# Norm factors spread by transposes, a shorter square-root chain, and latent norms taken half by half

## The chip, the cores and the metric

The kernel runs on one core of a Trainium2 chip. The metric is the device time in microseconds (us) of one execution of the whole program. A profile is taken of one execution, which has a time of its own.

## The reference

Two layers of a hybrid encoder are applied to 544 tokens (512 of a new stream, 32 of a running one). Cut to what matters here:

```
def rmsnorm(x, g):
    return x * rsqrt(mean(x * x, axis=-1) + EPS) * g

def mixer(h, ...):
    b_g, c_g, xin, q_lat, ckv, k_r, g_a, g_b = split(h @ w_in)
    y_a = (b_g * conv(c_g * xin)) @ w_conv_out
    q = rmsnorm(q_lat, norm_q) @ w_uq        # 384 features; then RoPE on a part
    c_new = rmsnorm(ckv, norm_kv)            # 256 features; also an output
    y_b = attention(q, c_new @ w_ukv, rope(k_r)) @ w_attn_out
    return (sigmoid(g_a) * y_a + sigmoid(g_b) * y_b) @ w_merge

def layer(x, ...):
    x = x + rmsnorm(mixer(rmsnorm(x, norm_attn_pre)), norm_attn_post)
    f = (silu(gate(h2)) * up(h2)) @ w_down   # h2 = rmsnorm(x, norm_ffn_pre)
    return x + rmsnorm(f, norm_ffn_post)
```

So each layer has four norms over 1024 features and two over the latents (384 and 256 features). Each needs one factor 1/sqrt(mean square + EPS) per token.

## The kernel before

Features lie on the 128 partitions and tokens along the free dimension. The tokens are worked in two halves of TH = 272 columns (`hf` 0 and 1). A product of a weight tile with a half is three matmuls, since both operands are split into a high and a low part (L184: low part of the weights, L185: low part of the data, L186: both high parts). Weights come as raw tiles of 512 KB by DMA from SP's queue; ACT copies out the high part (L129) and DVE subtracts to get the low part (L130). A unit is one output tile of 128 features for one half: 8 input tiles times 3, that is 24 products of 272 columns.

Each layer begins with the input projection. Its first part, units (m, hf) with m = 0 to 7 for half 0 and then for half 1, makes the query latent (m = 0 to 2), the key and value latent (m = 3, 4) and more; `p1_evict` copies each unit out of PSUM and adds its squares to `accq` or `acck` of its half. Then come the convolution branch, RoPE, attention, merge, gate and up, and down.

A norm factor is made in two steps. `rsqrt_cols` (L231) takes accumulators of squares, 128 partitions by 272 tokens. Three products per accumulator with one column of `ones` (L237, at token offsets `TB3` = 0, 128, 144) put the sums over the features on the partitions as three columns. DVE scales them (L239), makes a first guess `y` by integer arithmetic on the bits (L242) and improves it by three Newton steps of three operations (L244 to L246), all on tiles 128 by 3 per accumulator. Then it multiplies the identity by each column: three diagonal tiles `dg` per accumulator (L251). `bcast` (L255) multiplies `ones` with these tiles (L259: 128, 128 and 16 columns) and so spreads the factor over all partitions in PSUM, where DVE uses it.

`first_chain` (L388) does this once per half for the input, and `post_chain` (L320) twice per half after the merge and after the down projection (the norm on the way out and the next one on the way in; after the last projection there is no next one): 16 single spreads into the bank ring `v`. `qk_norms` (L506) does all four latent accumulators at once, 12 columns, after unit (6, 1) of each layer's first part. Their four spreads, two in ring `s` and two in ring `t`, follow one another a little later (L635 to L648), ahead of the products that need the normalised latents.

The order of PE's, SP's and POOL's instructions is that of the code. For DVE and ACT it is that of the code in the first layer's first part and from the merge to the end of the next layer's first part; elsewhere a scheduler orders them. PSUM's eight banks are rings: `d` 3, `s` 2, `t` 2, `v` 1. In the first part the call for the next bank, `psd`, goes round through `d`, `s` and `t` in a fixed order, for units and for the columns of `rsqrt_cols` alike.

Of the kernel before, what the change touches and what calls it, by code (L numbers as in the profile page):

```python
# [11 lines left out]
ALU = mybir.AluOpType  # L12
AX = mybir.AxisListType

P = 128
NL = 2
T = 544
TH = 272
# [5 lines left out]
EPS = 1e-6  # L24
QSCALE2 = 96.0
# [3 lines left out]
TB3 = (0, 128, 144)  # L29
# [4 lines left out]
def kernel(  # L34
# [25 lines left out]
    pe, dve, act, pool = nc.tensor, nc.vector, nc.scalar, nc.gpsimd  # L60
# [22 lines left out]
    def small(shape, dt=F32, s="s"):  # L83
        return sp.tile(shape, dt, tag="s", name=nm(s))

    def tiny(shape, s="y"):
        return sp.tile(shape, F32, tag="y", name=nm(s), bufs=16)
# [143 lines left out]
    def rsqrt_cols(accs):  # L231
        n = 3 * len(accs)
        ps = psd(n)
        v = tiny([P, 12], "v")[:, :n]
        for i, (acc, scale, eps) in enumerate(accs):
            for b, o in enumerate(TB3):
                pe.matmul(ps[:, 3 * i + b : 3 * i + b + 1], lhsT=acc.t[:, o : o + P], rhs=ones[:, 0:1], start=True, stop=True)  # L237
        for i, (acc, scale, eps) in enumerate(accs):
            dve.tensor_scalar(v[:, 3 * i : 3 * i + 3], ps[:, 3 * i : 3 * i + 3], scale, eps, op0=ALU.mult, op1=ALU.add)  # L239
        y = tiny([P, 12], "y")[:, :n]  # L240
        t = tiny([P, 12], "t")[:, :n]
        dve.tensor_scalar(y.bitcast(I32), v.bitcast(I32), -0.5, float(0x5F3759DF), op0=ALU.mult, op1=ALU.add)  # L242
        for _ in range(3):
            dve.tensor_mul(t, y, y)  # L244
            dve.scalar_tensor_tensor(t, t, -0.5, v, op0=ALU.mult, op1=ALU.mult)
            dve.scalar_tensor_tensor(y, t, 1.5, y, op0=ALU.add, op1=ALU.mult)  # L246
        out = []
        for i in range(len(accs)):
            d = small([P, TH], s="dg")
            for b, (o, a) in enumerate(((0, 0), (P, 0), (2 * P, 112))):  # L250
                dve.tensor_scalar_mul(d[:, o : min(o + P, TH)], ident[:, a:P], y[:, 3 * i + b : 3 * i + b + 1])  # L251
            out.append(d)
        return out

    def bcast(d, tag="v"):  # L255
        ps = bank(tag)[:, :TH]
        for o in (0, P, 2 * P):
            e = min(o + P, TH)
            pe.matmul(ps[:, o:e], lhsT=ones, rhs=d[:, o:e], start=True, stop=True)  # L259
        return ps  # L260

    FS = 1.0 / (NC * P)
# [190 lines left out]
    for l in range(NL):  # L453
# [26 lines left out]
        accq = [Acc(), Acc()]  # L480
# [20 lines left out]
                if m < 5:  # L501
                    (accq if m < 3 else acck)[hf].add(dst)

        qk = []

        def qk_norms():  # L506
            qk.extend(rsqrt_cols([(acck[0], 1.0 / 256, EPS), (acck[1], 1.0 / 256, EPS),
                                  (accq[0], QSCALE2 / 384, EPS * QSCALE2), (accq[1], QSCALE2 / 384, EPS * QSCALE2)]))

        if l == 0:  # L510
            pend = []

            def evict(n):
                for _ in range(n):
                    p1_evict(*pend.pop(0))
# [9 lines left out]
                (7, 0): lambda: evict(1),  # L525
                (1, 1): lambda: (next(norm_b), next(norm_a)),
                (3, 1): lambda: (next(norm_b), evict(4)),
                (4, 1): lambda: evict(1),
                (5, 1): lambda: evict(1),
                (6, 1): lambda: (evict(1), qk_norms()),  # L530
                (7, 1): lambda: (evict(1), next(norm_b)),
            }

# [11 lines left out]
        else:  # L545
            pend = []
            for m, hf, ps in win_tiles(range(8), 8, P1Src(h, raws)):
                pend.append((m, hf, ps))
                if hf == 0 or hf in sready:
                    while pend:  # L550
                        p1_evict(*pend.pop(0))
                tick()
                if (m, hf) == (6, 1):
                    qk_norms()
            while 1 not in h:
                step()
            while loaded:
# [645 lines left out]
```

## Time and profile before

| what | us |
|---|---|
| three runs: lowest, median, highest | 2022.95, 2024.89, 2026.08 |
| the profiled execution | 2026.63 |
| its span, first to last instruction | 2024.6 |
| PE busy in the span | 1992.8 |
| DVE busy in the span | 1147.1 |

The profiled execution took 2.0 us more than its span, and 1.74 us more than the median of the runs. PE has work in nearly the whole span. Its mean granted clock is 0.994 of full speed.

### The profile page before, as it was taken

What the parts mean: (1) busy time and instruction counts of PE and PEld (TensorE: products, weight loads), DVE (VectorE), ACT (ScalarE), POOL (GpSimd) and SP (SyncE); (2) the same over time, 40 slices, a digit from 0 to 9 for tenths busy, and PEclk for the clock granted to TensorE, in tenths of its full rate; (3) what the DMA queues carried; (4) which work ended last, traced back from release to release, by engine and by line L of the source; (5) the groups of instructions that cost most, each with busy time, mean ns of one, the idle gap of its engine ahead of it and who ended that gap; (6) DMA issues with size and microseconds to landing.
All of it is one profiled execution on the core that took longest, in us unless ns stands there. A gap on an engine that the chain in (4) does not pass through costs nothing.

```text
span 2024.6 us, 37375 instructions
## 1 busy us (share of the span) xinstructions
PE 1992.8 (98%) x15588; PEld 1970.8 (97%) x15588; DVE 1147.1 (57%) x2410; ACT 827.2 (41%) x1676; POOL 85.7 (4%) x212
## 2 busy tenths in 40 slices
PE   8999999999999999999999999999999999999997
PEld 8999999999999999999999999999999999999997
DVE  7877776534467444422668777864344664444234
ACT  5455555622353223222444555556123533222231
POOL 0100000000000000000100100100000000000000
PEclk9999999999999999999999999999999999999998
DMA  5122222222342222232532222222223412222233
GB/s 192 62 77 68 69 82 69 92 97 84 116 150 84 84 84 84 84 97 86 184 105 77 65 65 75 88 83 88 84 94 118 158 55 93 85 95 81 79 115 125
DMA packets 58890, 190.92 MB, mean 94 GB/s; under 512 B 7969, under 2 KB 9665, under 8 KB 58593
## 3 DMA queue, kind: packets, MB, share of 16 engines
q1 hardware_dynamic: 49104, 163.58, 24.1%
q0 software_dynamic: 8320, 22.66, 3.4%
q8 instruction: 122, 2.00, 0.4%
q10 hardware_dynamic: 1296, 2.29, 0.3%
q14 instruction: 48, 0.39, 0.1%
HBM read 174.11 MB, written 10.20 MB: 91 GB/s over the span
## 4 chain that ended last, share of the span: by engine, by line
PE 93%; DVE 4%; DMA 1%; ACT 1%; issue 1%; SPq 0%; DVEq 0%; ACTq 0%
PE ps_d L184 16%; PE ps_d L186 16%; PE ps_d L185 16%; PE ps_s L184 7%; PE ps_s L186 7%; PE ps_s L185 7%; PE ps_t L184 6%; PE ps_t L186 6%; PE ps_t L185 6%; PE ps_t L757 2%; DMA raw<-in_w_in 1%; PE ps_v L772 1%; PE ps_v L773 1%; DVE w L130 1%; ACT w L129 1%
## 5 line engine op out<-in xcount | busy, mean ns | idle before, releaser
L130 DVE TENSOR_TENSOR w<-raw,w 128x1024 fp32r<-128x1024 f32 (+4 forms) x317 | 363.8, 1148 | 433.5 <-ACT w L129 432.5
L129 ACT CAST w<-raw 128x1024 fp32r<-128x1024 f32 (+4 forms) x317 | 312.1, 986 | 263.3 <-PE ps_d L186 109.4
L184 PE MATMUL ps_d<-hh,w 128*128 128x272 f32 x1080 | 314.9, 292 | 1.3 <-DVE v L130 1.3
L185 PE MATMUL ps_d<-hl,w 128*128 128x272 f32 x1080 | 312.0, 289 | 0.8 <-DVE hl L314 0.8
L186 PE MATMUL ps_d<-hh,w 128*128 128x272 f32 x1080 | 312.1, 289 | 0.0
L184 PE MATMUL ps_d<-gh,w 128*128 128x272 f32 x704 | 205.9, 292 | 6.0 <-DVE w L130 6.0
L184 PEld LDWEIGHTS ps_d<-hh,w 128*128 128x128 f32 x1080 | 203.8, 189 | 3.0 <-PE ps_d L186 1.7
L185 PEld LDWEIGHTS ps_d<-hl,w 128*128 128x128 f32 x1080 | 203.5, 188 | 2.0 <-DVE hl L314 1.3
L186 PE MATMUL ps_d<-gh,w 128*128 128x272 f32 x704 | 204.5, 291 | 0.0
L185 PE MATMUL ps_d<-gl,w 128*128 128x272 f32 x704 | 203.5, 289 | 0.0
L186 PEld LDWEIGHTS ps_d<-hh,w 128*128 128x128 f32 x1080 | 203.1, 188 | 0.0
L184 PEld LDWEIGHTS ps_d<-gh,w 128*128 128x128 f32 x704 | 133.3, 189 | 6.5 <-DVE w L130 6.3
L184 PE MATMUL ps_s<-gh,w 128*128 128x272 f32 x464 | 136.9, 295 | 1.1 <-DVE w L130 1.1
L186 PE MATMUL ps_s<-gh,w 128*128 128x272 f32 x464 | 136.1, 293 | 0.0
L185 PE MATMUL ps_s<-gl,w 128*128 128x272 f32 x464 | 135.4, 292 | 0.0
L185 PEld LDWEIGHTS ps_d<-gl,w 128*128 128x128 f32 x704 | 133.6, 190 | 0.0
L186 PEld LDWEIGHTS ps_d<-gh,w 128*128 128x128 f32 x704 | 133.3, 189 | 0.0
L184 PE MATMUL ps_t<-gh,w 128*128 128x272 f32 x432 | 125.5, 290 | 0.0
L186 PE MATMUL ps_t<-gh,w 128*128 128x272 f32 x432 | 125.0, 289 | 0.0
L185 PE MATMUL ps_t<-gl,w 128*128 128x272 f32 x432 | 124.3, 288 | 0.0
L1051 ACT ACTIVATE sl<-sl 128x272 f32<-128x272 f32 x88 | 38.0, 432 | 183.2 <-DVE sl L1050 182.0
L1059 ACT CAST fh<-sl 128x272 fp32r<-128x272 f32 x88 | 36.9, 420 | 162.1 <-DVE sl L1057 162.1
(330 smaller groups left out, 5410.0 us busy)
## 6 DMA issues: line engine op xcount, KB each, us to landing
raw<-in_w_in SPq DMA_DIRECT2D x91, 512.0 KB, 3.2
raw<-in_w_gu SPq DMA_DIRECT2D x88, 512.0 KB, 3.2
raw<-in_w_mix SPq DMA_DIRECT2D x48, 512.0 KB, 3.2
raw<-in_w_dn SPq DMA_DIRECT2D x36, 512.0 KB, 3.5
raw<-in_w_dn SPq DMA_DIRECT2D x18, 384.0 KB, 3.0
raw<-in_w_b SPq DMA_DIRECT2D x16, 320.0 KB, 2.8
x_mid<-xb POOLq DMA_DIRECT2D x16, 272.0 KB, 2.3
xb<-x_mid POOLq DMA_DIRECT2D x16, 272.0 KB, 4.4
```

The costliest lines, as they stand in the source:

```text
L129: act.copy(hi, src)
L130: dve.tensor_sub(lo, src, f32(hi))
L184: pe.matmul(ps, lhsT=wlo, rhs=xhi, start=first, stop=False)
L185: pe.matmul(ps, lhsT=whi, rhs=xlo, start=False, stop=False)
L186: pe.matmul(ps, lhsT=whi, rhs=xhi, start=False, stop=last)
L757: pe.transpose(pt[:, o * P : o * P + P], probs[qt][:, kt * P : kt * P + P], ident)
L772: pe.matmul(out, lhsT=both, rhs=ptl[:, b, o : o + 256], start=kt == 0, stop=False)
L773: pe.matmul(out, lhsT=both, rhs=pth[:, b, o : o + 256], start=False, stop=kt == nkt - 1)
L1051: act.activation(sl, sl, AF.Silu)
L1059: act.copy(fh[:, i % 8, :], sl)
```

## The change

`bcast` no longer multiplies. It transposes: each of the three columns of `y`, repeated 128 times by a stride of zero, is the stationary operand, the identity goes through, and 128 columns come out. The third transpose overlaps the second. The diagonal tiles and their DVE operations are gone. The chain after the first guess has 7 operations on small tiles in place of 9: a third-order step of four and a Newton step of three, with constants folded. `qk_norms` is called per half, on two accumulators (6 columns): half 0 after unit (4, 1) in layer 0 and after unit (2, 1) in layer 1, half 1 after unit (6, 1) in both. Each call takes a bank of its own, so the banks of later units in the first part shift by one.

```diff
         t = tiny([P, 12], "t")[:, :n]
+        u = tiny([P, 12], "u")[:, :n]
         dve.tensor_scalar(y.bitcast(I32), v.bitcast(I32), -0.5, float(0x5F3759DF), op0=ALU.mult, op1=ALU.add)
-        for _ in range(3):
-            dve.tensor_mul(t, y, y)
-            dve.scalar_tensor_tensor(t, t, -0.5, v, op0=ALU.mult, op1=ALU.mult)
-            dve.scalar_tensor_tensor(y, t, 1.5, y, op0=ALU.add, op1=ALU.mult)
-        out = []
-        for i in range(len(accs)):
-            d = small([P, TH], s="dg")
-            for b, (o, a) in enumerate(((0, 0), (P, 0), (2 * P, 112))):
-                dve.tensor_scalar_mul(d[:, o : min(o + P, TH)], ident[:, a:P], y[:, 3 * i + b : 3 * i + b + 1])
-            out.append(d)
-        return out
-
-    def bcast(d, tag="v"):
+        dve.tensor_mul(t, y, y)
+        dve.tensor_mul(t, t, v)
+        dve.scalar_tensor_tensor(u, t, -10.0 / 3.0, t, op0=ALU.add, op1=ALU.mult)
+        dve.scalar_tensor_tensor(y, u, 5.0, y, op0=ALU.add, op1=ALU.mult)
+        dve.tensor_mul(t, y, y)
+        dve.scalar_tensor_tensor(t, t, -27.0 / 1024.0, v, op0=ALU.mult, op1=ALU.mult)
+        dve.scalar_tensor_tensor(y, t, 0.5625, y, op0=ALU.add, op1=ALU.mult)
+        return [y[:, 3 * i : 3 * i + 3] for i in range(len(accs))]
+
+    def bcast(y, tag="v"):
         ps = bank(tag)[:, :TH]
-        for o in (0, P, 2 * P):
-            e = min(o + P, TH)
-            pe.matmul(ps[:, o:e], lhsT=ones, rhs=d[:, o:e], start=True, stop=True)
+        for b, o in enumerate(TB3):
+            pe.transpose(ps[:, o : o + P], y[:, b : b + 1].to_broadcast([P, P]), ident)
         return ps
...
-        qk = []
-
-        def qk_norms():
-            qk.extend(rsqrt_cols([(acck[0], 1.0 / 256, EPS), (acck[1], 1.0 / 256, EPS),
-                                  (accq[0], QSCALE2 / 384, EPS * QSCALE2), (accq[1], QSCALE2 / 384, EPS * QSCALE2)]))
+        qk = {}
+
+        def qk_norms(hf):
+            qk[hf], qk[2 + hf] = rsqrt_cols([(acck[hf], 1.0 / 256, EPS), (accq[hf], QSCALE2 / 384, EPS * QSCALE2)])
...
-                (4, 1): lambda: evict(1),
+                (4, 1): lambda: (evict(1), qk_norms(0)),
                 (5, 1): lambda: evict(1),
-                (6, 1): lambda: (evict(1), qk_norms()),
+                (6, 1): lambda: (evict(1), qk_norms(1)),
...
                 tick()
+                if (m, hf) == (2, 1):
+                    qk_norms(0)
                 if (m, hf) == (6, 1):
-                    qk_norms()
+                    qk_norms(1)
```

On PE in layer 0, the 24 one-column products over the four accumulators `acc` stand together before the change, between the products of unit (6, 1) and those of unit (7, 1), as do 24 more at the same place of layer 1. The names are tile names with buffer numbers; `gh` and `gl` are the data's high and low parts.

```order
L186 MATMUL ps_t_88_706<-gh_98,w_325 128x272
L237 MATMUL ps_d_90_734<-ones,acc_411 128x1 x3
L237 MATMUL ps_d_90_734<-ones,acc_678 128x1 x3
L237 MATMUL ps_d_90_734<-ones,acc_370 128x1 x3
L237 MATMUL ps_d_90_734<-ones,acc_645 128x1 x3
L184 MATMUL ps_s_98_780<-gh_98,w_363 128x272
```

With the change, the same place has 12 of them. A row with x3 stands for the three products of one accumulator.

```order
L186 MATMUL ps_d_93_717<-gh_98,w_320 128x272
L237 MATMUL ps_s_95_745<-ones,acc_668 128x1 x3
L237 MATMUL ps_s_95_745<-ones,acc_635 128x1 x3
L184 MATMUL ps_t_100_766<-gh_98,w_358 128x272
```

The other 12 stand two units earlier, after unit (4, 1).

```order
L186 MATMUL ps_d_84_640<-gh_98,w_249 128x272
L237 MATMUL ps_s_87_670<-ones,acc_406 128x1 x3
L237 MATMUL ps_s_87_670<-ones,acc_365 128x1 x3
L184 MATMUL ps_t_92_691<-gh_98,w_285 128x272
```

What moved: one block of 24 became two blocks of 12 with two units between them, in banks of another ring.

The second place is the four spreads of the latents on PE in layer 0. Before, each is three products of `ones` with a diagonal tile.

```order
L259 MATMUL ps_s_123_948<-dg_764,ones 128x128 x2
L259 MATMUL ps_s_123_948<-dg_764,ones 128x16
L259 MATMUL ps_s_124_956<-dg_768,ones 128x128 x2
L259 MATMUL ps_s_124_956<-dg_768,ones 128x16
L259 MATMUL ps_t_125_964<-dg_772,ones 128x128 x2
L259 MATMUL ps_t_125_964<-dg_772,ones 128x16
L259 MATMUL ps_t_130_981<-dg_776,ones 128x128 x2
L259 MATMUL ps_t_130_981<-dg_776,ones 128x16
```

After, each is three transposes of 128 columns.

```order
L186 MATMUL ps_d_121_905<-hh_543,w_901 128x272
L256 MATMUL ps_s_125_934<-ident,y_680 128x128 x3
L256 MATMUL ps_s_126_942<-ident,y_755 128x128 x3
L256 MATMUL ps_t_127_950<-ident,y_680 128x128 x3
L256 MATMUL ps_t_132_967<-ident,y_755 128x128 x3
L184 MATMUL ps_d_138_997<-hh_793,w_901 128x272
```

What moved: nothing, but 12 PE operations with another stationary operand stand in the place of 12.

The third place is DVE in layer 0, somewhat later, where the scheduler sets the order. `qf` is a normalised query tile, `qn` its low part, `w` a weight tile of 1024 columns, `cns` a low part of the cached latent. Before:

```order
L130 TENSOR_TENSOR qn_985<-qf_990,qn_985 128x272
L646 SCALAR_TENSOR_TENSOR qf_994<-lat_167,gn,ps_t_130_981 128x272
L473 TENSOR_TENSOR ue_911<-cs_944,ps_d_140_1043 128x272
L130 TENSOR_TENSOR qn_985<-qf_994,qn_985 128x272
L475 TENSOR_TENSOR ue_911<-cs_1036,ps_d_141_1069 128x240
L476 TENSOR_TENSOR ue_911<-cs_1036,ps_d_141_1069 128x32
L130 TENSOR_TENSOR w_1200<-raw_1199,w_1200 128x1024
L130 TENSOR_TENSOR cns_1102<-ps_t_144_1103,cns_1102 32x256
```

After:

```order
L130 TENSOR_TENSOR qn_971<-qf_976,qn_971 128x272
L470 TENSOR_TENSOR ue_897<-cs_930,ps_d_142_1029 128x272
L644 SCALAR_TENSOR_TENSOR qf_980<-lat_167,gn,ps_t_132_967 128x272
L472 TENSOR_TENSOR ue_897<-cs_1022,ps_d_143_1055 128x240
L473 TENSOR_TENSOR ue_897<-cs_1022,ps_d_143_1055 128x32
L130 TENSOR_TENSOR w_1186<-raw_1185,w_1186 128x1024
L130 TENSOR_TENSOR cns_1088<-ps_t_146_1089,cns_1088 32x256
L130 TENSOR_TENSOR qn_971<-qf_980,qn_971 128x272
```

What moved: the last low part of the query's second half stands behind the weight tile and `cns`, no longer ahead of them.

## Rows read from the trace of the kernel before

**Rows 1.** Page, part 1: busy us, share of the span, instructions of each engine.
```profile
PE 1992.8 (98%) x15588; PEld 1970.8 (97%) x15588; DVE 1147.1 (57%) x2410; ACT 827.2 (41%) x1676; POOL 85.7 (4%) x212
```

**Rows 2.** Waits of PE: line, releaser: us in total, times, longest us.
```profile
PE ps_d L184 <- DVE w L130: 6.0, 2, 5.7
PE ps_v L259 <- DVE dg L251: 5.5, 2, 2.8
```

**Rows 3.** Timeline of PE at a single spread: start us, us, what.
```profile
22.84 0.73 PE L259 MATMUL ps_v<-dg,ones 128*128 128x128 f32 x6
23.43 0.37 PE L184 MATMUL ps_t<-gh,w 128*128 128x272 f32 x1
```

**Rows 4.** Timeline of PE at layer 0's four latent spreads.
```profile
76.01 1.41 PE L259 MATMUL ps_s<-dg,ones 128*128 128x128 f32 x12
...
78.61 0.37 PE L184 MATMUL ps_d<-hh,w 128*128 128x272 f32 x1
```

**Rows 5.** Timeline of PE at two sets of attention transposes.
```profile
112.28 0.93 PE L757 MATMUL ps_t<-ident,pr 128*128 128x128 f32 x7
112.97 0.37 PE L184 MATMUL ps_d<-hh,w 128*128 128x272 f32 x1
...
122.47 0.49 PE L757 MATMUL ps_t<-ident,pr 128*128 128x128 f32 x3
122.72 0.48 PE L184 MATMUL ps_d<-c,w 128*128 128x512 f32 x1
```

**Rows 6.** Windows: stretch us, PE, PEld, DVE, ACT, POOL, granted clock, DMA, GB/s.
```profile
58.12:60.71 2.59, 2.59 (x26) 2.59 (x25) 1.25 (x4) 0.00 (x0) 0.00 (x0) 1.00 0.00 0
60.71:65.33 4.62, 4.62 (x27) 4.62 (x27) 4.06 (x26) 0.00 (x0) 0.00 (x0) 0.63 0.00 0
112.97:115.99 3.02, 3.02 (x27) 3.02 (x26) 2.14 (x3) 1.72 (x3) 0.00 (x0) 1.00 0.00 0
1013.54:1015.87 2.33, 0.85 (x9) 0.70 (x7) 1.48 (x3) 0.00 (x0) 0.00 (x0) 1.00 0.71 264
1024.14:1028.76 4.62, 4.62 (x28) 4.62 (x27) 4.62 (x7) 1.24 (x2) 0.00 (x0) 0.63 0.43 138
1063.37:1066.46 3.09, 3.09 (x26) 3.09 (x25) 3.06 (x8) 0.93 (x2) 0.00 (x0) 0.83 0.00 0
1066.46:1072.05 5.59, 5.59 (x25) 5.59 (x26) 4.47 (x27) 0.00 (x0) 0.00 (x0) 0.50 0.00 0
```

**Rows 7.** Timeline of DVE and PE at the layers' boundary; in brackets idle before, releaser.
```profile
1019.75 1.23 DVE L130 TENSOR_TENSOR w<-raw,w 128x1024 fp32r<-128x1024 f32 x1 [1.09 <-ACT w L129]
1020.89 0.15 DVE L239 TENSOR_SCALAR v<-ps_d 128x3 f32<-128x3 f32 x1
...
1022.85 0.16 DVE L246 SCALAR_TENSOR_TENSOR y<-t,y 128x3 f32<-128x3 f32 x1
1023.05 0.63 DVE L251 TENSOR_SCALAR dg<-ident,y 128x128 f32<-128x128 f32 x3
1023.48 0.81 PE L259 MATMUL ps_v<-dg,ones 128*128 128x128 f32 x6 [2.84 <-DVE dg L251]
```

**Rows 8.** Timeline of DVE and PE at the last spread of the program.
```profile
2012.23 0.16 DVE L239 TENSOR_SCALAR v<-ps_d 128x3 f32<-128x3 f32 x1 [0.92 <-PE ps_d L237]
...
2014.82 1.43 PE L259 MATMUL ps_v<-dg,ones 128*128 128x128 f32 x6 [2.63 <-DVE dg L251]
2016.29 1.35 DVE L335 TENSOR_TENSOR m<-m,ps_v 128x544 f32<-128x544 f32 x2 [1.28 <-PE ps_v L259]
```

**Rows 9.** Timeline of DVE and PE in layer 0, 86 to 97 us.
```profile
86.82 0.44 DVE L130 TENSOR_TENSOR qn<-qf,qn 128x272 fp32r<-128x272 f32 x1
...
89.04 1.23 DVE L130 TENSOR_TENSOR w<-raw,w 128x1024 fp32r<-128x1024 f32 x1 [0.58 <-ACT w L129]
...
89.98 0.28 PE L185 MATMUL ps_d<-qn,w 128*128 128x272 f32 x1
...
90.19 0.41 DVE L130 TENSOR_TENSOR cns<-ps_t,cns 32x256 fp32r<-32x256 f32 x1
...
96.71 0.70 DVE L425 TENSOR_TENSOR xr<-xr,sh 128x544 f32<-128x544 f32 x1
```

**Rows 10.** Line L259: duration ns min/median/max, first and last start us, forms.
```profile
L259 PE MATMUL ps_v<-dg,ones x96: 182/273/553, 22.8 to 2015.9; 128*128 128x128 f32 x64, 128*128 128x16 f32 x32
L259 PE MATMUL ps_s<-dg,ones x24: 182/274/356, 76.0 to 1082.4; 128*128 128x128 f32 x16, 128*128 128x16 f32 x8
L259 PE MATMUL ps_t<-dg,ones x24: 182/275/356, 77.3 to 1083.7; 128*128 128x128 f32 x16, 128*128 128x16 f32 x8
```

## The prediction, made before the changed kernel was run

> **What bounds the kernel now.** I read the page's first part: PE is busy for 1992.8 of 2024.6 us, DVE for 57% of them [rows 1]. So PE's own order of products sets the end, and an edit is worth what it takes out of PE's stream, out of PE's waits, or gives back of its clock. DVE work as such is worth nothing, unless PE waits for it. Next the waits of PE: two of them are for the diagonal tiles of a spread, 5.5 us [rows 2]. Then the timeline of PE at every place that the change touches. There I measure a stretch from the start of its first product to the start of the product behind it, since products overlap and their durations do not add up. Last the windows over one unit of 24 products each, with the granted clock: a unit takes 3.02 us at clock 1.00 [rows 6], which is the level of 2.4 GHz; at 0.50, 1.2 GHz, it takes 5.59 us [rows 6].
>
> **Single spreads.** One takes from 22.84 to 23.43, that is 0.59 us [rows 3], and there are 16 of them: 96 rows of six (a product of 32-bit data leaves two rows) [rows 10]. The trace of before has no transpose of a step-0 column, but it has transposes of 128 columns in attention: three rows take 0.25 us and seven rows 0.69, so about 0.08 to 0.10 each [rows 5]. From below a transpose could cost as little as 0.08; from above as much for a column as the two-row products that it replaces, 0.59 x 128 / 272 = 0.28 us, since its data are 32 bits wide as well. I take 0.10, because the attention transposes also have identity, 128 columns and 32-bit data; only the stride differs. A spread is then 0.28 to 0.30, and saves 0.3. Of the 16, 12 stand where PE is busy without a gap: 12 x 0.31 = **3.7**. Two more, ahead of the wait at the boundary of the layers, count nothing, since PE there waits 1.48 us or more for DVE and DMA anyway (it is busy for 0.85 of the 2.33 us from 1013.54) [rows 6]. The last two are counted below, with their waits. With the upper price a spread would take 0.84 and lose 0.25.
>
> The diagonal tiles that go, three for each spread, free DVE 0.63 us per spread [rows 7]; at 57% busy this is under PE's cover and counts only where PE waits for it.
>
> **The two sets of four spreads.** From 76.01 to 78.61, 2.60 us [rows 4], and as much in layer 1. Twelve transposes at 0.10 are 1.2. Saved: 2 x 1.4 = **2.8**.
>
> **The clock.** Ahead of the latent norms stand 24 one-column products in a row, 2.59 us at clock 1.00. The next unit takes 4.62 us at a mean clock of 0.63 [rows 6]. In layer 1 the block itself takes 3.09 at 0.83 and the next unit 5.59 at 0.50 [rows 6]. So a clock of 2.4 GHz fell to 1.2 GHz behind 2.6 us of products of a single column. The change halves the block: 12 products, about 1.3 us, then two units of full products, then 12 more. A stretch that I can set beside it is 1013.54 to 1015.87: 2.33 us with PE busy for only 0.85, and the clock stayed at 1.00 [rows 6]. That is less activity for a longer time than 12 such products, so I expect no fall. Gain: 4.62 - 3.02 = 1.6 in layer 0, 5.59 - 3.02 + 3.09 - 2.59 = 3.1 in layer 1, together **4.7**. If the clock falls all the same, the gain is 0 or less.
>
> Here stands a reason to doubt the transposes. [Rows 5, 6] show seven of them, and the unit behind them at 1.00 in 3.02 us. The Trainium skill ("TensorE: Matmul & The Clock Gate", section "Part 4: PE-mode transpose") says that a transpose does not count as busy time for the clock in the way a product does; by that, twelve in a row could do to the clock what the one-column products did, and 2 x 1.6 of the gain would be lost, for a sum of 10.0 in place of 13.2. The row has seven transposes and not twelve, so it does not exclude this. By my price the twelve last 1.2 us, half of the block that did lower it.
>
> **The boundary of the layers.** PE waits 2.84 us and starts its spread at 1023.48 [rows 7]. Ahead of it is a chain on DVE alone, which begins at 1020.89 behind a wide weight split: 11 small operations, one each 0.196 us ((1022.85 - 1020.89) / 10), then the diagonal tiles [rows 7]. Two operations fewer are 0.39, and PE no longer waits for the first tile. From the end of the last small operation (1022.85 + 0.16) to PE's start lies 0.47; with three tiles in 0.63 one takes 0.21 or more, and two DVE operations follow each other with a gap of 0.04, so the tile's part is between 0.21 and 0.43, and I take 0.34. PE starts 0.73 earlier, and the spread is 0.3 shorter: **1.0**. Behind this wait the clock falls: the next unit takes 4.62 us at 0.63 [rows 6], 1.6 more than at 1.00. The idle stretch gets shorter, from 3.0 to 2.3 us, as short as the one that left the clock alone, so I count half: **0.8**.
>
> **The tail.** The last spread waits 2.63 us for the same chain, starts at 2014.82 and is read at 2016.29, 1.47 later, at the low clock [rows 8]. The chain is 0.73 shorter. By 0.30 to 0.59 the spread would halve; the handover in it stays, so I take 0.45. **1.2**, all of it on the path, since nothing is behind it but the last tiles.
>
> **What is new: a wait in layer 0.** The scheduler puts the last low part of the query behind the weight split and `cns`. In the trace before, the product that reads that low part starts at 89.98, the split starts at 89.04 and takes 1.23, `cns` starts at 90.19 [rows 9]. After the change the low part would start where `cns` is followed by the next DVE operation, about 90.53, and end 0.44 later [rows 9], at 90.95. PE would be there at 89.98: **1.0 lost**. The split waits for a copy that waits for PE, so it comes earlier with PE and the wait keeps its size. Between 0, if the split happens to slip in earlier, and 1.4. Behind it on DVE come RoPE's operations and a split; they begin 0.4 later, which PE's own delay covers. The other reordered rows, RoPE's sum that ends the sequence at 96.71 [rows 9] among them, come no later than they are needed.
>
> **The banks.** In the first part each unit now finds another bank. The units' evictions have been done for long where the ring comes round; only one meets its bank within 0.1 us. I count nothing; the cover is the two units between a bank's eviction and its next use, and each missed one would cost tenths.
>
> **Sum:** 3.7 + 2.8 + 4.7 + 1.0 + 0.8 + 1.2 - 1.0 = 13.2. The profiled execution took 2026.63, so it would take 2013.4. It lies 1.74 above the median of the three runs, 2024.89. Executions differ by up to 3.1 us, and the lost clock, which is the part that the change mostly takes away, may well be what differs, so I subtract half of the 1.74: **2012.6**.
>
> **Rivals.** (1) *The clock falls at the half blocks too.* For it: one-column products did lower it, and twelve are still a disturbance; the granted clock in [rows 6] went down in layer 1 within the block itself. Against it: the stretch at 1013.54. Then 4.7 is not gained: 2017.3. If both half blocks lower it, in both layers, another 3.2 is lost, 2020.5.
> (2) *The transposes do not pay.* Either they lower the clock (the skill's rule above), worked out here from rows as two units at 4.62 in place of 3.02: 2012.6 + 3.2 = 2015.8. Or a column costs what it costs in the products (the upper price): 3.7, 2.8 and 0.7 of the boundary and the tail go, and 22 spreads lose 0.25 each, 5.5: 2025.3. Rows of the same shape at 0.10 speak against this, so of the 0.12 it gets 0.03.
> (3) *The stationary operand of stride zero is slow to load, and the kernel gets slower.* No row of before shows such a load. With 22 spreads on PE's path (12 single, eight latent, boundary, tail) there are 66 transposes; 12.3 us are to be eaten up for the old median, 0.19 each on top of 0.10, and 16.3 (0.25 each on top) to be slower by 4 us. So it decides from about 0.35 us for one transpose, some 3.5 times the price of those in [rows 5]. At 0.4 the time is 2012.6 + 66 x 0.3 = 2032. Against it: the weights' columns come through the same path, whatever they hold, and the load of the next operand lies beside the running product (PEld is busy as long as PE [rows 1]).
> (4) *The change does not do what it says:* the chain of waits is as long as before because something else ends last at the boundary and in the tail, and PE's cheaper stream is used up by DVE splits that are now late. With PE at 98% [rows 1] there is little room for that: 2021 to 2025.
>
> **How the numbers follow.** Chances: forecast 0.66, rival 1 0.12, rival 2 0.12, rival 3 0.05, rival 4 0.05. The predicted time is the forecast's. Its own range is 2009.5 to 2015.5: below, the boundary's clock in full (0.8), no new wait (1.0), the rest of the offset (0.9) and cheaper transposes (0.08 for 0.10, some 1); above, no part of the offset subtracted (0.9), the boundary's clock not at all (0.8), and a new wait of 1.4. For 8 in 10 it has to take in rival 1 and the first case of rival 2, each with some 1 us to spare: **2009.5 to 2018.5**. What a measurement of this kernel can tell from no change is about 0.2%, 4 us: faster means below 2020.8. The forecast, rival 1 and the first case of rival 2 lie there, and a little of rival 4: 0.66 + 0.12 + 0.09 + 0.02 = 0.89. The rest of rival 4, the second case of rival 2 and what of rival 3 stops short of 0.35 us: same 0.07. The rest of rival 3: slower 0.04.
>
> **What would show it.** Right: the row of a single spread on PE with three transposes and the next product 0.3 us later; twelve transposes in 1.2 us; clock 1.00 in the units behind the one-column products of both layers; PE's waits for `dg` replaced by waits of some 2.1 us for `y`; the last small operation of the chain two places shorter; a new wait of PE for the query's low part in layer 0, of about 1 us. Wrong: a granted clock of 0.5 behind the half blocks or behind the twelve transposes, transposes above 0.25 us, waits of PE in the first part for a bank that ACT or DVE has not emptied, or DVE's splits named in more of PE's waits than before.

## The result and the profile after

Four runs of the changed kernel took 2012.29 to 2013.14 us, median 2012.78. The runs of the kernel before in the same comparison had a median of 2024.72. The ratio is 0.9941, with a 95% interval of 0.9924 to 0.9959. The prediction was 2012.6, and the range held it. Ten more runs of the changed kernel in two later comparisons (below) had means of 2014.07 and 2014.82, with ratios of 0.9955 (0.9942 to 0.9969) and 0.9958 (0.9945 to 0.9970). So the gain is 9 to 12 us, and the first comparison was at its upper end. All 14 runs of the changed kernel together lie between 2012.29 and 2017.49, with a mean of 2013.96; 55 runs of the kernel before lie between 2021.17 and 2026.71, with a mean of 2023.47. From mean to mean the gain is 9.5 us.

The profiled execution after took 2012.29 us, span 2010.4. The page's first part answers to [rows 1] (PEld is TensorE's loading of stationary operands, which overlaps PE):

```profile
PE 1980.8 (99%) x15516; PEld 1958.1 (97%) x15516; DVE 1130.5 (56%) x2318; ACT 826.1 (41%) x1676; POOL 86.1 (4%) x212
```

PE lost 12.0 us of busy time and 72 rows; DVE lost 16.6 us. The waits of PE (us in total, times, longest) answer to [rows 2]. The wait for `dg` is now one for `y` and 3.0 us shorter, and a new one stands beside it, for the query's low part:

```profile
PE ps_d L184 <- DVE w L130: 6.0, 1, 6.0
...
PE ps_v L256 <- DVE y L250: 2.5, 2, 1.9
...
PE ps_d L185 <- DVE qn L130: 0.8, 1, 0.8
```

The timeline of PE at the same single spread as in [rows 3] and at the four latent spreads of [rows 4]:

```profile
22.40 0.29 PE L186 MATMUL ps_s<-gh,w 128*128 128x272 f32 x1
22.53 0.49 PE L256 MATMUL ps_v<-ident,y 128*128 128x128 f32 x3
22.78 0.38 PE L184 MATMUL ps_t<-gh,w 128*128 128x272 f32 x1
...
73.54 0.82 PE L256 MATMUL ps_s<-ident,y 128*128 128x128 f32 x6
74.19 0.82 PE L256 MATMUL ps_t<-ident,y 128*128 128x128 f32 x6
74.77 0.37 PE L184 MATMUL ps_d<-hh,w 128*128 128x272 f32 x1
```

A spread goes from 22.53 to 22.78: 0.25 us where it was 0.59. Four go from 73.54 to 74.77: 1.23 where they were 2.60. The windows (us, PE, PEld, DVE, ACT, POOL, granted clock, DMA, GB/s) over the four half blocks of one-column products, with the unit behind two of them, and then over three stretches at the boundary of the layers, answer to [rows 6]:

```profile
51.09:52.34 1.25, 1.25 (x14) 1.25 (x13) 1.25 (x4) 0.46 (x3) 0.00 (x0) 1.00 0.00 0
...
58.48:59.73 1.25, 1.25 (x14) 1.25 (x13) 0.92 (x3) 0.00 (x0) 0.00 (x0) 1.00 0.00 0
59.73:62.84 3.11, 3.11 (x26) 3.11 (x26) 1.57 (x10) 0.00 (x0) 0.00 (x0) 1.00 0.00 0
...
1043.93:1045.19 1.26, 1.26 (x15) 1.26 (x13) 0.00 (x0) 0.00 (x0) 0.98 (x2) 1.00 0.00 0
...
1057.70:1058.96 1.26, 1.26 (x15) 1.26 (x13) 1.26 (x4) 0.74 (x3) 0.00 (x0) 1.00 0.00 0
1058.96:1061.98 3.02, 3.02 (x26) 3.02 (x26) 2.83 (x12) 0.20 (x1) 0.00 (x0) 1.00 0.00 0
1009.49:1011.87 2.38, 0.85 (x8) 0.69 (x7) 1.53 (x3) 0.00 (x0) 0.00 (x0) 1.00 0.69 262
1011.87:1014.41 2.54, 2.54 (x15) 2.54 (x14) 1.01 (x1) 1.76 (x3) 0.00 (x0) 0.58 0.49 171
1014.41:1018.01 3.60, 3.60 (x25) 3.53 (x24) 2.33 (x8) 1.77 (x4) 0.00 (x0) 0.82 0.47 152
```

The clock is 1.00 behind every half block (the two units that are not shown took 3.11 us each). At the boundary it falls behind 1009.49 to 1011.87. That is the same stretch of work as 1013.54 to 1015.87 in [rows 6], which had left the clock alone in the profile before.

The products of 272, 256 and 512 columns are the same in both kernels, and in the same order, so their starts can be compared one by one. Each entry of this table is the time between the same two products in a kernel less that in the first profile of the kernel before (the stretches are named by that profile's times). The tail is the time from the last product's start to the end of the span. The rows below the first two belong to the experiments.

| kernel | 50 to 70, latent norms L0 | 70 to 79, four spreads | 79 to 100, query | 570 to 700, four single spreads | 985 to 1030, boundary | 1048 to 1073, latent norms L1, one single spread | 1073 to 1086, four spreads | tail |
|---|---|---|---|---|---|---|---|---|
| changed kernel | -1.51 | -1.35 | +1.12 | -1.06 | -2.74 | -3.40 | -1.37 | -1.63 |
| before, second profile | -0.07 | 0.01 | -0.01 | 0.00 | -1.70 | -3.07 | 0.01 | 0.00 |
| changed, 2nd and 3rd profile | -1.51, -1.50 | -1.37, -1.38 | +1.12, +1.12 | -1.06, -1.06 | -2.15, -2.40 | -3.40, -3.40 | -1.37, -1.37 | -1.28, -1.27 |
| joint norms, two profiles | -1.50, +0.02 | -1.38, -1.38 | +1.12, +1.12 | -1.07, -1.05 | -2.99, -1.96 | -1.87, -3.41 | -1.37, -1.37 | -1.63, -1.63 |
| halves only | +0.34 | 0.02 | 0.01 | 0.01 | -1.62 | -3.06 | 0.01 | 0.00 |
| transposes only | -1.50 | -1.35 | +1.11 | -1.06 | -2.48 | -0.34 | -1.38 | -0.89 |
| chain only | 0.01 | 0.00 | 0.00 | -0.01 | -1.56 | -1.56 | 0.00 | -0.39 |
| query first, two profiles | -1.51, -1.50 | -1.37, -1.36 | +0.30, +0.01 | -1.05, -1.05 | -2.97, -2.45 | -3.41, -3.41 | -1.37, -1.37 | -1.27, -1.28 |

### The profile page after: what moved, and what is told of

It reads as the page before. It is cut to its first block, busy times and chain, and to the rows that moved or that the text cites. A ratio compares the mean times of both kernels' runs of the same rounds, so it can differ in the third digit from the quotient of the medians.

```text
span 2010.4 us, 37143 instructions
## 1 busy us (share of the span) xinstructions
PE 1980.8 (99%) x15516; PEld 1958.1 (97%) x15516; DVE 1130.5 (56%) x2318; ACT 826.1 (41%) x1676; POOL 86.1 (4%) x212
## 4 chain that ended last, share of the span: by engine, by line
PE 92%; DVE 4%; DMA 1%; ACT 1%; issue 1%; DVEq 0%; SPq 0%; ACTq 0%
PE ps_d L184 16%; PE ps_d L186 16%; PE ps_d L185 16%; PE ps_s L184 7%; PE ps_s L186 7%; PE ps_s L185 7%; PE ps_t L184 6%; PE ps_t L186 6%; PE ps_t L185 6%; PE ps_t L755 2%; DMA raw<-in_w_in 1%; PE ps_v L770 1%; DVE w L130 1%; PE ps_v L771 1%; ACT w L129 1%
## 5 line engine op out<-in xcount | busy, mean ns | idle before, releaser
L184 PE MATMUL ps_d<-hh,w 128*128 128x272 f32 x1096 | 320.0, 292 | 1.3 <-DVE v L130 1.3
L185 PE MATMUL ps_d<-hl,w 128*128 128x272 f32 x1096 | 317.0, 289 | 0.8 <-DVE hl L311 0.8
L186 PE MATMUL ps_d<-hh,w 128*128 128x272 f32 x1096 | 317.3, 290 | 0.0
L184 PEld LDWEIGHTS ps_d<-hh,w 128*128 128x128 f32 x1096 | 206.9, 189 | 3.0 <-PE ps_d L186 1.7
L186 PEld LDWEIGHTS ps_d<-hh,w 128*128 128x128 f32 x1096 | 206.6, 189 | 0.0
L184 PE MATMUL ps_t<-gh,w 128*128 128x272 f32 x464 | 135.0, 291 | 0.0
L186 PE MATMUL ps_t<-gh,w 128*128 128x272 f32 x464 | 134.2, 289 | 0.0
L185 PE MATMUL ps_t<-gl,w 128*128 128x272 f32 x464 | 133.6, 288 | 0.0
L184 PE MATMUL ps_s<-gh,w 128*128 128x272 f32 x432 | 125.4, 290 | 0.1
L186 PE MATMUL ps_s<-gh,w 128*128 128x272 f32 x432 | 125.0, 289 | 0.0
L185 PE MATMUL ps_s<-gl,w 128*128 128x272 f32 x432 | 124.4, 288 | 0.0
```

The costliest lines, as they stand in the source:

```text
L184: pe.matmul(ps, lhsT=wlo, rhs=xhi, start=first, stop=False)
L185: pe.matmul(ps, lhsT=whi, rhs=xlo, start=False, stop=False)
L186: pe.matmul(ps, lhsT=whi, rhs=xhi, start=False, stop=last)
```

## Experiments

Theory A at first was the prediction's: each part pays for itself on PE's path, and the block's length decides the clock. The rivals are in the expectations, under letters of their own. Twelve runs of nine kernels follow.

**The parts by themselves.** The first undoes the calls per half in the changed kernel; the other three put one part each into the kernel before.

```diff
 joint_norms: the changed kernel, with
+        qk.extend(rsqrt_cols([(acck[0], ...), (acck[1], ...), (accq[0], ...), (accq[1], ...)]))   # at (6, 1)
 halves_only: the kernel before, with
+        qk[hf], qk[2 + hf] = rsqrt_cols([(acck[hf], ...), (accq[hf], ...)])   # at (4, 1) or (2, 1), and (6, 1)
 transposes_only: the kernel before, with
+            pe.transpose(ps[:, o : o + P], y[:, b : b + 1].to_broadcast([P, P]), ident)   # no dg
 chain_only: the kernel before, with the seven operations in place of the nine
```

> The changed kernel with the latent norms of both halves together again (24 one-column products in a row, one chain of 12 columns); transposes and short chain stay. Theory A (the length of the block decides the clock): the granted clock falls to 0.5 behind the block in both layers as in the kernel before, 1.6 and 3.1 us are lost again, so 2012.8 + 4.6 = 2017.4 us; the wait for the query's low part in layer 0 stays at 1.0 us, since DVE's order there is that of the changed kernel. Theory B (the clock falls at moments that shift with anything in PE's stream, and halving the block has nothing to do with it): clock 1.00 behind at least one of the two blocks, 2012.5 to 2015.

> The kernel before with only the latent norms of the halves apart (products with diagonal tiles and the chain of nine operations stay). Theory A (the length of the block decides the clock): clock 1.00 behind all four half blocks, 4.6 us faster than before, 2020.1 us; no wait for the query's low part in layer 0, since DVE's order there is that of the kernel before. Theory B (the clock falls at moments that shift with anything): some of the units behind the blocks still at 0.5, 2022 to 2025.

> The kernel before with only the spreads by transposes (no diagonal tiles; the chain of nine operations and the joint latent norms stay). Theory A (each part pays for itself on PE's path): ten single spreads at 0.34 = 3.4, the sets of four 2.7, the first diagonal tile and the spread at the boundary 0.7, in the tail 0.3 + 0.4 to 0.9, less 1.1 for the wait in layer 0, whose DVE order this part alone brings: 6.5 to 7 us faster, 2017.8 us, clock behind the joint blocks 0.5 as before; another 1.5 if the clock at the layers' boundary falls inside the wait. Theory C (the transposes gain little, the clock and the chain made the difference): single spreads not shorter than 0.5 us, 2022 to 2025.

> The kernel before with only the shorter chain (seven operations for nine); diagonal tiles and joint latent norms stay. Theory A (DVE operations count only where PE waits for them): 2 x 0.196 at the boundary and 2 x 0.196 in the tail, 0.8 us faster, 2023.9 us, not to be told from no change. Theory D (the chain is what matters, as every norm waits for it): 16 chains at 0.4 and two at the latents, 7 us faster, 2017.7.

Measured, against 21 runs of the kernel before with a mean of 2023.17:

```
joint_norms      mean 2015.16 (2013.23 to 2017.63,  5 runs)  ratio 0.9960 (0.9948 to 0.9973)
halves_only      mean 2022.61 (2021.60 to 2025.68, 11 runs)  ratio 0.9998 (0.9989 to 1.0006)
transposes_only  mean 2015.22 (2013.64 to 2016.62,  5 runs)  ratio 0.9959 (0.9945 to 0.9972)
chain_only       mean 2021.83 (2020.26 to 2024.72, 11 runs)  ratio 0.9992 (0.9983 to 1.0001)
```

The transposes carry most of the gain: 8.0 us on the means, beside 1.3 for the chain and 0.6 for the halves, 9.9 together, and the whole change gains 9.5. Theories C and D are out. Theory A is right on the spreads (0.34 and 1.37 in the table) and on the wait in layer 0 (+1.11 and +1.12 in these kernels with transposes, 0.01 or less in those without). On the clock neither A nor B held. The joint block of the first experiment left the clock at 1.00 in layer 0 and lowered it in layer 1 for less long than before (the unit behind it took 4.54 us at 0.65, where it had been 5.59 at 0.50). The transposes alone came out 2.6 us below the 2017.8 that A gave; in their profile the joint block of layer 0 did not lower the clock, and the stretch there gained 1.50, which A had not counted. The halves alone, forecast 4.6 us faster, gained nothing that can be measured. Yet their four blocks all kept 1.00. Two things had to be found out: what a joint block does to the clock from one execution to the next, and why the halves alone gain nothing in layer 0 (+0.34 in the table).

**The length of a block, and many transposes.** One kernel is the changed one as it is, one does each one-column product of the latent norms twice, one repeats transposes.

```diff
 double_columns:
-            for b, o in enumerate(TB3):
-                pe.matmul(ps[:, 3 * i + b : 3 * i + b + 1], lhsT=acc.t[:, o : o + P], rhs=ones[:, 0:1], start=True, stop=True)
+            for b, o in enumerate(TB3 * (2 if len(accs) > 1 else 1)):
+                c = 3 * i + b % 3
+                pe.matmul(ps[:, c : c + 1], lhsT=acc.t[:, o : o + P], rhs=ones[:, 0:1], start=True, stop=True)
 more_transposes:
-        for b, o in enumerate(TB3):
-            pe.transpose(ps[:, o : o + P], y[:, b : b + 1].to_broadcast([P, P]), ident)
+        for _ in range(2 if tag == "v" else 4):
+            for b, o in enumerate(TB3):
+                pe.transpose(ps[:, o : o + P], y[:, b : b + 1].to_broadcast([P, P]), ident)
```

> The changed kernel as it is, beside the next three. Theory A2 (a block of 24 one-column products lowers the clock in a part of the executions, a block of 12 in none, and that is what makes the executions of the kernel before differ by 5 us): all executions within 1 us, 2012.3 to 2013.3, mean clock 0.997 in each. Theory B (the clock falls at moments that shift with anything): executions differ by 3 us or more, as those of the kernel before and of the one with joint norms do.

> The changed kernel with every one-column product of the latent norms done twice, 24 in a row in four blocks. 48 products more at 0.107 us (2.59 / 24): 5.1 us, 2017.9. Theory A2: the clock falls behind some of the four blocks, the executions differ by 3 us or more again, 2018 to 2024. Theory B (the length of a block decides nothing): clock 1.00 behind all four, 2017.5 to 2018.5, the executions within 1 us.

> The changed kernel with each single spread's transposes done twice and those of the latents four times, 48 in a row. Theory A (a transpose costs 0.08 to 0.10 us, the granted clock stays through any number of them): ten single spreads 0.24 each, boundary and tail 0.3 each, 3.0; 72 transposes more at the latents 7.3; less 1.0, as DVE's order in layer 0 here has the query's low part ahead of the weight split: 2012.8 + 9.3 = 2022. Theory E (the rule of the Trainium skill, page TensorE: Matmul & The Clock Gate, Part 4, that transposes don't count as busy time for the clock): the granted clock falls to 0.5 within or behind the 4.9 us of transposes in both layers, another 3 to 10 us, 2025 to 2032.

Measured, against 21 runs of the kernel before with a mean of 2023.54:

```
after_again      mean 2014.07 (2012.77 to 2015.53,  5 runs)
double_columns   mean 2023.32 (2020.54 to 2025.74, 11 runs)
more_transposes  mean 2024.65 (2022.93 to 2028.07, 11 runs)
```

The changed kernel's own executions differ by 2.8 us, not by 1, and with the last five runs below by 5.2, nearly as much as the 5.5 of the kernel before. Yet its clock fell behind no half block in any of its three profiles. The run of 2017.49 has no profile, but its mean granted clock is 0.996, as that of the run of 2013.25. So A2 fails in this part: falls behind the blocks are not all that makes executions differ. All 14 runs of the changed kernel have a mean clock of 0.996 or 0.997; of the 51 runs of the kernel before in the later comparisons, those at 0.994 or less all took 2023.59 or more. A part of the spread of the kernel before goes with the clock; what spreads the runs of the changed kernel is open. The windows of double_columns over its four blocks of 24, three of them with the unit behind:

```profile
51.16:53.76 2.60, 2.60 (x27) 2.60 (x25) 2.10 (x6) 1.07 (x4) 0.00 (x0) 1.00 0.03 6
...
59.89:62.51 2.62, 2.62 (x26) 2.62 (x25) 0.88 (x2) 0.00 (x0) 0.00 (x0) 0.99 0.00 0
62.51:67.12 4.61, 4.61 (x26) 4.61 (x26) 1.56 (x10) 0.00 (x0) 0.00 (x0) 0.63 0.00 0
1048.60:1051.19 2.59, 2.59 (x26) 2.59 (x25) 0.00 (x0) 0.00 (x0) 1.58 (x4) 1.00 0.00 0
1051.19:1055.82 4.63, 4.63 (x27) 4.63 (x27) 1.56 (x10) 0.00 (x0) 0.00 (x0) 0.63 0.00 0
1065.21:1067.81 2.60, 2.60 (x27) 2.60 (x25) 2.60 (x7) 0.95 (x3) 0.00 (x0) 1.00 0.00 0
1067.81:1070.90 3.09, 3.09 (x26) 3.09 (x26) 2.17 (x12) 0.00 (x0) 0.00 (x0) 1.00 0.00 0
```

Two of the four lowered the clock, two did not. So A2 holds for the blocks: the same products, doubled to 24 in a row, bring back the falls. The forecast of B, 1.00 behind all four, does not hold. The mean lies 9.4 us above the changed kernel's 2013.96: 5.1 for the products, as forecast, and 3.0 for two falls of 1.5 as in the profile; 1.3 was not placed. The windows of more_transposes over its 48 transposes in layer 0 and in layer 1, with the stretch behind each:

```profile
75.22:80.38 5.16, 5.16 (x51) 5.16 (x49) 4.97 (x13) 3.02 (x6) 0.49 (x1) 1.00 0.31 102
80.38:83.41 3.03, 3.03 (x27) 3.03 (x25) 3.03 (x8) 2.06 (x5) 0.56 (x2) 1.00 0.53 207
1080.09:1085.25 5.16, 5.16 (x50) 5.16 (x49) 3.79 (x10) 2.03 (x4) 1.05 (x2) 1.00 0.19 69
1085.25:1088.20 2.95, 2.95 (x26) 2.95 (x25) 2.95 (x9) 1.71 (x5) 0.00 (x0) 1.00 0.52 204
```

Four times as many transposes as the change has, 5.16 us of them, and the clock stays at 1.00. That is twice as long as the 24 one-column products, which lowered it in some executions. Theory E is out. The price: 36 more took 5.16 - 1.23 = 3.93 us, 0.109 each, and three more in a single spread 0.33. The mean lies 2.6 us above the 2022 that A gave: 0.6 is the price at the sets of four (2 x 3.93 for 7.3), 0.9 that at ten single spreads (0.33 for 0.24), and the rest was not placed. In the profiled execution, one of the two slowest at 2027.92, the boundary of the layers took 3.1 us or more longer than in the changed kernel's profiles (+0.94 by the measure of the table's column): PE waits 3.5 us for `y` there, where it was 0.6 or less, and the clock falls behind that wait.

**The wait in layer 0.** The query latent is written ahead of the key and value latent, the code of both unchanged.

```diff
         for hf in range(2):
-            r = bcast(qk[hf], "s")       # key and value
...
-        for hf in range(2):
             r = bcast(qk[2 + hf], "t")   # query
...
+        for hf in range(2):
+            r = bcast(qk[hf], "s")
...
```

> The changed kernel with the query latent's spreads, scalings and splits written ahead of those of the key and value latent; DVE's order in layer 0 then has the query's last low part ahead of the weight split again. Theory A (the wait at the query's low part is what the change loses in layer 0): that wait gone, 1.0 us faster than the changed kernel, 2011.7. Rival F (DVE has that much work there in any order): PE waits as long for the key and value latent's low part or for a weight split instead, 2012.8.

Mean 2012.08 (2010.54 to 2013.24), ratio 0.9944 (0.9932 to 0.9957), beside 2014.07 for the changed kernel. The waits of PE from 78 to 100 us, first in the changed kernel:

```profile
PE ps_d L185 <- DVE qn L130: 0.8, 1, 0.8
PE ps_d L184 <- DVE v L130: 0.7, 1, 0.7
```

And in the one with the query first:

```profile
PE ps_d L184 <- DVE v L130: 0.9, 1, 0.9
```

The wait for `qn` is gone; 0.2 comes back at the next one. Theory A holds, F does not.

**Once more.** The last runs asked how much of the clock's loss an execution of the kernel before has, whether the halves are worth anything beside the transposes, and whether the version with the query first is faster.

> The kernel before as it is, for a second profile of it. Theory A2 (a block of 24 one-column products lowers the clock in a part of the executions): behind the two blocks not the same stretches at 0.5 as in the first profile (3.4 us in layer 0, 6.8 in layer 1), and the span differs by what they cost; from 2019 to 2024 us. Theory G (the first profile shows what every execution does): the same three stretches, span 2024.6.

> Once more the changed kernel with the latent norms of both halves together, beside the changed kernel in the same call, since five executions of each did not tell them apart (2014.1 against 2014.0, but means of 2015.2 and 2014.1). Theory A2: on the mean 1 to 2.5 us slower than the changed kernel, with executions up to 2017.6. Theory H (taking the halves apart is worth nothing once the spreads are transposes): the same mean within 0.5 us.

> The changed kernel as it is, beside the kernels of this call: 2012.3 to 2015.5 us, as in the nine executions so far.

> Once more the changed kernel with the query latent written first, beside the changed kernel in the same call. Theory A: 0.8 to 1.4 us faster than the changed kernel on the mean, 2011.5 to 2012.5, as the trace shows 1.0 us less wait at the query's low part and 0.3 given back behind it. Rival F: the same within 0.5 us, and the first result was chance.

```
before_again     2021.45 (one run, with a profile); nine other runs of it 2022.01 to 2025.31
joint_norms_2    mean 2015.98 (2014.28 to 2019.99, 5 runs)  ratio 0.9963 (0.9951 to 0.9976)
after_3          mean 2014.82 (2013.45 to 2017.49, 5 runs)  ratio 0.9958 (0.9945 to 0.9970)
q_first_2        mean 2012.88 (2012.41 to 2013.32, 5 runs)  ratio 0.9949 (0.9935 to 0.9962)
```

In the second profile of the kernel before, the windows over layer 0's block of 24, the unit behind it and the three units after that, then over layer 1's block and the unit behind it, are these:

```profile
57.63:60.23 2.60, 2.60 (x27) 2.60 (x25) 1.25 (x4) 0.00 (x0) 0.00 (x0) 1.00 0.00 0
60.23:63.34 3.11, 3.11 (x27) 3.11 (x27) 2.56 (x17) 0.00 (x0) 0.00 (x0) 1.00 0.00 0
63.34:75.47 12.13, 10.55 (x75) 9.47 (x74) 12.13 (x32) 4.79 (x10) 1.80 (x4) 1.00 0.01 2
1060.90:1063.49 2.59, 2.59 (x26) 2.59 (x25) 2.59 (x7) 0.94 (x2) 0.00 (x0) 1.00 0.00 0
1063.49:1066.60 3.11, 3.11 (x26) 3.11 (x26) 2.70 (x17) 0.00 (x0) 0.00 (x0) 1.00 0.00 0
```

No fall behind either block, so G is out: the first profile, with the lower mean clock (0.994, the second has 0.996) and a time of 2026.63 at the upper end of the 55 runs, is not what every execution does. Over all profiles, a block of 24 was followed by a fall in 9 of 16 cases (six profiles with two joint blocks each, double_columns with four blocks), a block of 12 in none of 28 (seven profiles with four each).

The third row shows the other half of the riddle. The three units took 12.13 us, against 10.68 in the first profile, with DVE busy all the time in both. The first profile's row:

```profile
65.33:76.01 10.68, 9.85 (x73) 9.30 (x73) 10.68 (x24) 4.80 (x10) 1.69 (x4) 1.00 0.01 2
```

What the unit behind the block gains in clock, 1.5 us, PE gives back in waits for the two parts of the normalised input, `hh` and `hl`: of the 1.51 us by which its products started earlier behind that unit, 0.08 are left at 68.71. The waits of PE in this stretch, then the one in the first profile's stretch:

```profile
PE ps_d L185 <- DVE hl L314: 1.2, 3, 0.4
PE ps_d L184 <- ACT hh L309: 0.2, 1, 0.2
...
PE ps_d L185 <- DVE hl L314: 0.8, 2, 0.4
```

These parts are made behind the chain and its 12 diagonal tiles on DVE (here from the second profile):

```profile
62.85 2.21 DVE L251 TENSOR_SCALAR dg<-ident,y 128x128 f32<-128x128 f32 x12
```

So in the kernel before, DVE is the bound here, whatever the clock does: -0.07 without a fall. Without the tiles PE gains the 1.5 us, with joint blocks too (-1.50 for transposes only and for one profile of joint norms), but only where the clock stays. In the other profile of joint norms it fell in layer 0, and the stretch gained nothing (+0.02):

```profile
60.06:64.67 4.61, 4.61 (x26) 4.61 (x26) 1.74 (x12) 0.00 (x0) 0.00 (x0) 0.63 0.00 0
```

With halves apart and tiles kept, PE gains nothing either (+0.34). So the 1.5 us of layer 0 need both: no tiles and no fall.

Joint norms against the changed kernel: 2015.57 on the mean of ten runs, 2013.96 on the mean of fourteen. The difference of 1.6 is as A2 expects, but with standard deviations of 2.2 and 1.4 us between executions its own error is 0.8. H is unlikely, not excluded.

The query first is faster than the changed kernel in both comparisons: means of 2012.08 and 2012.88 beside 2014.07 and 2014.82, and 1.5 us below the mean of all 14 runs. The trace shows 0.8 to 1.1 of these 1.5 to 2 us; where the rest is from is open.

## Why the prediction was right, and where it was not

**Spreads.** Right: 0.34 for a single one (predicted 0.31) and 1.36 for a set of four (1.4). Of the 12 that were to count, ten did. The other two, one at each layer's merge (at 583.78 and 1588.03 in the first profile), were given back but for 0.07 at the sum of squares of the norm behind it: there 0.83 us lie between the starts of two products before and 1.10 after, as PE now waits for that sum. So the 3.7 came to 3.5. A zero-stride column costs no more than the attention's data (0.25 us for three, as in [rows 5]); rival 3 had no part.

**The clock, 4.7.** This is the term that was mis-sized, though the sum against the first profile fitted (-1.51 in layer 0, -3.06 in layer 1 without its single spread). It took one execution's falls for those of all. In layer 1 they cost 3.1 us in two of the six profiles with joint blocks, 1.5 in two and nothing in two, 1.5 on the mean; the halves alone moved the mean of the runs by 0.6 (2023.17 to 2022.61), less than can be told from nothing. In layer 0 the fall cost nothing in the kernel before, since PE would have waited for DVE instead. The 1.5 us there come only when the diagonal tiles are gone as well. Of them the prediction had said that they count only where PE waits for DVE; it had not seen that this is such a place, because the first profile hid the wait under the slow clock. The expectation that 12 products leave the clock alone was right, 28 times in 28. But its argument was not: the stretch set beside it, 1013.54 to 1015.87 in [rows 6], was followed by a fall in the changed kernel's first profile.

**The offset.** The prediction subtracted half of the 1.74 us by which the profiled execution lay above the median, because the change takes the lost clock away. That counts it twice: what the change removes was in the sum already. Without it the forecast would be 2013.4, nearer to the mean of 14 runs, 2013.96. The bounds of the prediction's own range, 2009.5 and 2015.5, are not quite what its list adds up to: 3.7 below and 2.1 above would be 2008.9 and 2014.7. The medians and means measured, 2012.78 and 2013.96, lie between either pair.

**The boundary, 1.0 + 0.8.** The first term was right. The chain began at 1020.89 and PE's spread at 1023.48 before [rows 7]; after, this is

```profile
1016.83 0.15 DVE L239 TENSOR_SCALAR v<-ps_d 128x3 f32<-128x3 f32 x1
...
1018.41 0.16 DVE L250 SCALAR_TENSOR_TENSOR y<-t,y 128x3 f32<-128x3 f32 x1
...
1018.72 0.51 PE L256 MATMUL ps_v<-ident,y 128*128 128x128 f32 x3 [0.55 <-DVE y L250]
1018.98 0.37 PE L184 MATMUL ps_t<-hh,w 128*128 128x272 f32 x1
```

that is 1.89 in place of 2.59, and 0.26 to the next product in place of 0.66: 1.1 in all. The second term is not the change's. The kernels without transposes gained 1.6 to 1.7 in this stretch as well, the kernel before itself among them, since only the first profile had the fall behind the wait. Between the layers 13 of the 14 profiles have one or two falls of 3.4 us, but not in the same place. Those that come ahead of the wait bring PE to it late, and the wait takes up what they cost or a part of it. That is why the wait for `y` here is 0.55, 0 and 0.51 us in the three profiles of the changed kernel, and not the 2.1 that the prediction named as a sign; in the first profile with the query first, where the fall lay some 18 us further ahead, it is 1.81. With 2.4 for the mean of the changed kernel's three profiles, 2.4 - 1.6 = 0.8 is left for the change.

**The tail, 1.2.** Measured 1.63, 1.28, 1.27. The chain and the first tile gave 0.71 (PE's spread started at 2014.82 [rows 8], 4.71 after the last product, and 4.00 after it in the changed kernel). The spread took 1.47 before its reader started, and now

```profile
2001.53 0.51 PE L256 MATMUL ps_v<-ident,y 128*128 128x128 f32 x3 [1.92 <-DVE y L250]
2002.08 1.35 DVE L332 TENSOR_TENSOR m<-m,ps_v 128x544 f32<-128x544 f32 x2 [0.70 <-PE ps_v L256]
```

0.55, which is 0.92 less: together the 1.63. In this profile the clock fell only behind the spread; where it falls ahead of it, as in the other two, the tail gains 1.27 or 1.28.

**The new wait, 1.0.** Right, +1.12, and its cause as well: the transposes bring DVE's new order, and the order with the low part ahead takes most of it away. The timeline of DVE and PE there:

```profile
85.21 1.23 DVE L130 TENSOR_TENSOR w<-raw,w 128x1024 fp32r<-128x1024 f32 x1 [0.15 <-ACT w L129]
...
86.35 0.41 DVE L130 TENSOR_TENSOR cns<-ps_t,cns 32x256 fp32r<-32x256 f32 x1
86.69 0.42 DVE L130 TENSOR_TENSOR qn<-qf,qn 128x272 fp32r<-128x272 f32 x1
...
87.16 0.40 PE L185 MATMUL ps_d<-qn,w 128*128 128x272 f32 x1 [0.84 <-DVE qn L130]
```

**The rivals.** (1) did not happen. The rule weighed in (2) is that a transpose does not count as busy time for the clock in the way a product does (Trainium skill, "TensorE: Matmul & The Clock Gate", section "Part 4: PE-mode transpose"). It does not show in this kernel: 48 transposes of 32-bit data in a row left the granted clock at 1.00, so the sum by the row, not the one by the rule, was the right one. Nor did the upper price of (2) hold. (3) and (4) did not happen.

The total of the terms was 13.2 from the profile's own time. The first profile after shows 14.3; from the first profile before to the mean of 14 runs after it is 12.7. From mean to mean it is 9.5, as the first profile lay 3.2 above the mean of its kernel.

**Luck.** That 2012.6 lay within 0.2 us of the median of the first four runs was in part luck. The sum fell 1.1 short of the gain from the first profile before to the first one after, the offset of 0.9 made up for most of it, and the four runs lay at the lower end of what later were 14. As a gain, from the median of the three runs before, the forecast was 12.3; the means differ by 9.5.

## What to carry to other kernels

A loss that one profile shows behind a disturbance of the clock need not be there in every execution: before it is counted, take a second profile, and look where the profiled execution lies among the kernel's runs. Ask what would bound the stretch if the clock had not fallen, since a slow stretch on PE can hide the wait of PE for another engine. Work taken off an engine that is half busy is not free of value; look for the places where it stands in a row ahead of what PE needs next, and look again at the order in which the scheduler puts what is left.

## What was not expected of the hardware

The same program on the same data had its clock lowered behind the same block in one execution and not in the next: 24 one-column products, 2.6 us, were followed by 1.2 GHz in 9 of 16 cases; twelve of them, 1.25 us, in none of 28. A stretch of 2.3 us in which PE was busy for 0.85 left the clock at 1.00 in one profile and was followed by a fall in another. Transposes, 5.16 us without a break, did not lower it. The load of a stationary column of stride zero took 0.132 to 0.137 us, no longer than that of a stored tile for attention's transposes, and less than the 0.186 to 0.333 of `ones` for the products that went. So in these rows the repeated column adds nothing, and the shorter load is that of a transpose (ns, lowest, median, highest; first the changed kernel, then twice the kernel before):

```profile
L256 PEld LDWEIGHTS ps_v<-ident,y x48: 132/136/137, 22.4 to 2001.7; 128*128 128x128 f32 x48
...
L757 PEld LDWEIGHTS ps_t<-ident,pr x320: 137/140/144, 108.7 to 1347.5; 128*128 128x128 f32 x160
...
L259 PEld LDWEIGHTS ps_v<-dg,ones x96: 186/192/333, 22.7 to 2015.8; 128*128 128x128 f32 x96
```
